# Stick-breaking attention on one core: scores of two heads issued in turn, transposed weights copied by ScalarE, last exponential one step earlier

## The chip, the cores and the metric

The kernel runs on one core of a Trainium2 chip. Time is the device time of one execution in microseconds. TensorE is PE in the profile (its weight loads are PEld), VectorE is DVE, ScalarE is ACT, GpSimd is POOL, and SyncE (SP) only starts transfers. Each engine takes its instructions strictly in the order in which the program left them, and waits on semaphores for what others make.

## The reference, cut to what matters

A decoder trunk of two layers over 1024 tokens of width 1024. Layer 0 mixes an S5 state-space block and eight heads of stick-breaking attention (head size 64); layer 1 has a pooling mixer; both have a large MLP and a gated embedding. Only the attention of layer 0 is touched by the change:

```
z = einsum("bhqd,bhkd->bhqk", qb, kf) * scale          # 128 queries of one block
causal = key_pos[None, :] < q_pos[:, None]
log_beta = log_sigmoid(z)
log_1m_beta = where(causal, log_sigmoid(-z), 0)
tail = cumsum(log_1m_beta, axis=keys, reverse=True) - log_1m_beta
w = where(causal, exp(log_beta + tail), 0)
out = einsum("bhqk,bhkd->bhqd", w, v)
```

So each row of a block of 128 queries needs a running sum over its keys from the right, between two exponentials and a logarithm. What precedes attention makes q, k and v; what follows multiplies its output by the second half of the output weights.

## The kernel before

Nearly all matrix products are split: an fp32 operand becomes a high part (rounded to the fp32r form, by ScalarE, L446) and a low part (VectorE subtracts, L450), and three products replace one (L477). This makes TensorE, VectorE and ScalarE all busy throughout.

Attention (`attention`, L661) is a list of **units**. The tokens have two halves `hf` of 512, each with four blocks `i` of 128 queries; heads come in four pairs. In the first half a unit is both heads of a pair for one block (16 units, up to 512 keys for each head). In the second half a unit is a single head (32 units, 640 to 1024 keys). A unit passes through five stages:

- `scores` (L670): TensorE multiplies q and k into PSUM banks of 512 columns (L682), adds the causal mask in the last bank (L686), ScalarE copies each bank into the tile `zs` (L687); VectorE then makes -|z| in `na` (L688) and max(z, 0) in `rz` (L689).
- `softplus` (L692): ScalarE takes exp and log of `na` (L694, L695), VectorE runs the reversed running sum over it into `rz` (L698).
- `weights` (L700): VectorE subtracts `rz` from `zs` (L702), ScalarE takes the exponential (L703): the attention weights.
- `turned` (L705): TensorE transposes the weights, 128 columns at a time, four to a PSUM bank of the tag `b` (L712), and VectorE copies each bank into the old `na` tile (L713).
- `values` (L715): TensorE multiplies the transposed weights with v (L730), both heads in turn.

The loop at L735 sets how the stages of successive units overlap: in step n it issues `values` of unit n-4, `weights` and `turned` of unit n-3, `softplus` of n-1, `scores` of n, with a `yield` after `turned`, one after `scores` and one more. At each yield other work may be woven in (`weave`, L1404): the rest of the projections, the GLU of S5, the two halves of the output projection and a first slice of the MLP. The order that results is handed to a scheduler that keeps each engine's list but places instructions by its own estimate of when they can run; what stands in the lists is shown below, since it follows from the code only loosely.

A head has 64 rows, so its score product uses the upper or the lower half of TensorE's rows: `rows = slice(64 * o, 64 * o + 64)`. PSUM banks for scores come from the tags `z` (two banks) and, in the second half, `st` (one). The tiles `zs` and `na` share a pool of eight buffers (`at`), `rz` one of four (`wq`), the transposed weights wait in two banks `b`. Other work uses these pools too: `wq` and `at` take weights and activations of the next stages.

## Time and profile before

| | |
|---|---|
| runs of the kernel before | 2160.73, 2167.41, 2173.29 us, median 2167.41 |
| the profiled execution | 2161.73 us; its span from first to last instruction 2159.9 us |
| busy over the span | PE 2072.2 us, PEld 1624.3, DVE 1838.9, ACT 1142.2, POOL 132.1 |
| instructions | PE 9464, DVE 2443, ACT 1613 |
| score matmuls (L682) | first at 262.6 us, last at 594.6 us |
| copies of transposed weights (L713) | 88, from 281.0 to 618.8 us |

Attention thus lies between about 260 and 622 us, a sixth of the span. Before and after it the kernel is projections, MLP and pooling. A row of the profile names line, engine, operation and tiles (`b<-ident,zs`: written tile, then the tiles read), shapes, count, and then busy time and mean duration. The mean of a PE row holds the pipeline's latency, so two matmuls that follow each other overlap in it: what a matmul costs TensorE is the distance of its start to that of the next. A wait is written with the instruction that ended it. `PEclk` is the share of its full clock that TensorE was granted.

### The profile page before, as it was taken

The page shows a single profiled execution, that of the slowest core. Times are in us where ns is not written, and L with a number is a line of the kernel's source. Part 1 is how long each engine was busy: PE and PEld are TensorE (multiplying, and loading weights), DVE is VectorE, ACT ScalarE, POOL GpSimd, SP SyncE. Part 2 cuts the span into 40 slices and gives each one's busy share as a digit, 9 for nine tenths or more (in the row PEclk, how much of TensorE's full clock was granted, in tenths as well). Part 3 has the DMA queues.
Part 4 walks back from the last instruction along what each step waited for, and adds up shares of the span by engine and source line. Part 5 has one row for each costly group of instructions (what it writes and reads, how often), then busy time and mean ns, then how long its engine had stood idle before and what let it go on. Part 6 is the DMA issues. An engine that isn't in the chain of part 4 may idle for free.

```text
span 2159.9 us, 24772 instructions
## 1 busy us (share of the span) xinstructions
PE 2072.2 (96%) x9464; PEld 1624.3 (75%) x9464; DVE 1838.9 (85%) x2443; ACT 1142.2 (53%) x1613; POOL 132.1 (6%) x263
## 2 busy tenths in 40 slices
PE   7899999989998999999999999888999999999997
PEld 5676766656577888888888887566888888888886
DVE  8866578978879888998878978999697998879998
ACT  5133466756644563756356555533654656365662
POOL 3856000000000000000000000000000000000000
PEclk9998999989899999999999999998999999999999
DMA  4111111220024112102202122322111201211221
GB/s 151 55 55 55 55 49 32 71 83 30 15 76 138 37 59 69 59 30 78 78 8 71 59 88 69 98 77 99 59 48 41 79 33 56 78 54 34 69 69 59
DMA packets 44742, 136.25 MB, mean 63 GB/s; under 512 B 9552, under 2 KB 10704, under 8 KB 44624
## 3 DMA queue, kind: packets, MB, share of 16 engines
q1 hardware_dynamic: 44624, 134.67, 18.6%
q8 instruction: 74, 1.21, 0.2%
q14 instruction: 44, 0.36, 0.1%
HBM read 129.28 MB, written 4.19 MB: 62 GB/s over the span
## 4 chain that ended last, share of the span: by engine, by line
PE 75%; DVE 19%; ACT 3%; issue 2%; DMA 1%; POOL 0%; SPq 0%; DVEq 0%; ACTq 0%
PE mm L477 27%; PE z L477 15%; PE b L477 12%; PE av L477 6%; PE st L477 6%; DVE rz L698 2%; DVE X L863 2%; DVE w L450 2%; PE z L682 1%; PE av L730 1%; PE b L712 1%; PE z L428 1%; DVE xgl L529 1%; DVE acc L499 1%; DVE na L713 1%
## 5 line engine op out<-in xcount | busy, mean ns | idle before, releaser
L477 PE MATMUL mm<-xgh,w 128*128 128x512 f32 x912 | 300.0, 405 | 15.5 <-ACT w L446 6.2
L450 DVE TENSOR_TENSOR w<-q,w 128x1024 fp32r<-128x1024 f32 x204 | 246.8, 1217 | 0.3 <-ACT w L446 0.3
L446 ACT CAST w<-q 128x1024 fp32r<-128x1024 f32 x204 | 212.8, 1047 | 29.0 <-PE mm L477 14.8
L477 PEld LDWEIGHTS mm<-xgh,w 128*128 128x128 f32 x912 | 173.1, 192 | 62.5 <-issue 9.1
L446 ACT CAST hsh<-H 128x1024 fp32r<-128x1024 f32 x98 | 102.3, 1047 | 197.1 <-PE st L477 88.5
L477 PE MATMUL mm<-xgl,w 128*128 128x512 f32 x456 | 183.0, 401 | 0.0
L446 ACT CAST w<-wr 128x1024 fp32r<-128x1024 f32 x98 | 102.3, 1047 | 150.1 <-PE mm L477 97.9
L477 PE MATMUL z<-xsh,w 128*128 128x512 f32 x576 | 177.7, 390 | 0.0
L863 DVE TENSOR_TENSOR q<-q,q 128x1024 f32<-128x1024 f32 x114 | 137.0, 1219 | 14.0 <-DMA q<-in_w_down 9.5
L450 DVE TENSOR_TENSOR w<-wr,w 128x1024 fp32r<-128x1024 f32 x98 | 128.1, 1312 | 21.1 <-ACT w L446 9.7
L477 PE MATMUL mm<-hsh,w 128*128 128x512 f32 x448 | 137.9, 389 | 0.0
L477 PE MATMUL b<-xsh,w 128*128 128x512 f32 x448 | 137.9, 389 | 0.0
L450 DVE TENSOR_TENSOR hsl<-H,hsh 128x1024 fp32r<-128x1024 f32 x98 | 119.4, 1219 | 11.4 <-ACT hsh L446 11.3
L446 ACT CAST xsh<-X 128x1024 fp32r<-128x1024 f32 x72 | 75.6, 1050 | 98.2 <-PE st L477 51.2
L477 PEld LDWEIGHTS z<-xsh,w 128*128 128x128 f32 x576 | 108.1, 188 | 22.9 <-issue 0.5
L477 PE MATMUL mm<-xsh,w 128*128 128x512 f32 x400 | 123.8, 389 | 0.0
L450 DVE TENSOR_TENSOR xsl<-X,xsh 128x1024 fp32r<-128x1024 f32 x72 | 87.4, 1220 | 38.7 <-ACT xsh L446 38.2
L477 PE MATMUL z<-xsl,w 128*128 128x512 f32 x288 | 112.1, 389 | 0.0
L450 DVE TENSOR_TENSOR xsl<-xt,xsh 128x512 fp32r<-128x512 f32 x108 | 70.1, 685 | 42.5 <-ACT xsh L446 42.5
L477 PEld LDWEIGHTS mm<-xgl,w 128*128 128x128 f32 x456 | 87.9, 193 | 21.8 <-issue 4.1
L477 PE MATMUL b<-hsh,w 128*128 128x512 f32 x336 | 103.6, 389 | 0.0
L477 PE MATMUL z<-hsh,w 128*128 128x512 f32 x336 | 103.4, 389 | 0.0
(360 smaller groups left out, 4874.5 us busy)
## 6 DMA issues: line engine op xcount, KB each, us to landing
q<-in_w_up SPq DMA_DIRECT2D x56, 512.0 KB, 3.6
q<-in_w_down SPq DMA_DIRECT2D x56, 512.0 KB, 3.7
wr<-in_w_in SPq DMA_DIRECT2D x26, 512.0 KB, 3.6
wr<-in_w_out SPq DMA_DIRECT2D x16, 512.0 KB, 3.5
wr<-in_w_up SPq DMA_DIRECT2D x16, 512.0 KB, 3.5
wr<-in_w_down SPq DMA_DIRECT2D x16, 512.0 KB, 3.5
x<-in_x SPq DMA_DIRECT2D x15, 512.0 KB, 5.7
wr<-in_w_gate SPq DMA_DIRECT2D x15, 512.0 KB, 3.5
```

The source lines that it names most:

```text
L428: nc.tensor.matmul(py[:, m], X[rows, ri, m, :], ca[rows, 2 * m + ri].rearrange("p j h -> p (j h)"), start=False, stop=(ri == 1))
L446: nc.scalar.copy(out=hi, in_=src)
L450: e.tensor_tensor(out=lo, in0=src, in1=hi.bitcast(F32), op=ALU.subtract)
L477: self.nc.tensor.matmul(ps, a, b, start=(first and n == 0 and i == 0), stop=(last and n == K - 1 and i == 2), skip_group_check=going)
L499: e.tensor_tensor(out=self.acc[hf], in0=self.acc[hf], in1=sq, op=ALU.add)
L529: self.nc.vector.scalar_tensor_tensor(out=lo, in0=x, scalar=g, in1=hi.bitcast(F32), op0=ALU.mult, op1=ALU.subtract)
L682: nc.tensor.matmul(pz[:, 0:b1 - b0], self.q[hf][pair // 2][rows, pair % 2, i * P:(i + 1) * P], self.k[b0 // HT][pair // 2][rows, pair % 2, ...
L698: v.tensor_tensor_scan(out=rz[:, rev], data0=na[:, rev], data1=rz[:, rev], initial=0.0, op0=ALU.add, op1=ALU.add)
L712: nc.tensor.transpose(pt[:, (kb - k0) * P:(kb - k0 + 1) * P], zs[:, kb * P:(kb + 1) * P], self.ident)
L713: v.tensor_copy(out=wT[:, k0 * P:k1 * P], in_=pt[:, 0:(k1 - k0) * P])
L730: nc.tensor.matmul(self.avp[64 * o:64 * o + 64, i * P:(i + 1) * P], self.v[kb // 4 * 2 + pair // 2][:, kb % 4, cs], w[:, at * P:(at + 1) * ...
L863: (self.nc.vector if eng == "v" else self.nc.gpsimd).tensor_tensor(out=o, in0=a, in1=b, op=op)
```

## The change

Three things change in `attention`, for the 48 units in all; the arithmetic stays the same.

1. In the second half, `scores` now takes the units of both heads at once. For each bank of 512 keys the matmul of head 0 and that of head 1 are issued one after the other, as the first half did already. It is called in the step of head 0, so head 1's scores are issued one step earlier than before.
2. The copies out of the transposes' banks (`turned`) go to ScalarE instead of VectorE.
3. The stages are issued in another order: `turned` of unit n-3, a yield, then in the second half `values` of the pair n-4 and n-3 as soon as its second head is turned, `weights` of n-2 (before: n-3), `softplus` of n-1, `scores`. In the first half `values` of n-4 still opens the step.

```
-        def scores(unit):
-            hf, pair, i, hs = unit
+        def scores(new):
+
+            hf, pair, i, _ = new[0]
             N = (4 * hf + i + 1) * P
-            zs, na = (self.a([P, SEQ], nm)[:, 0:len(hs) * N] for nm in ("zs", "na"))
-            rz = self.t([P, SEQ], "wq", name="rz")[:, 0:len(hs) * N]
+            heads = []
+            for unit in new:
+                W = len(unit[3]) * N
+                zs, na = (self.a([P, SEQ], nm)[:, 0:W] for nm in ("zs", "na"))
+                state[unit] = zs, na, self.t([P, SEQ], "wq", name="rz")[:, 0:W], N
+                heads += [(o, zs[:, n * N:(n + 1) * N]) for n, o in enumerate(unit[3])]
             for b0 in range(0, N, HT):
...
-                pzs = [self.p([P, HT], next(banks[hf])) for _ in hs]
+                pzs = [self.p([P, HT], next(banks[hf])) for _ in heads]
...
-                for n, pz in enumerate(pzs):
+                for pz, (_, zs) in zip(pzs, heads):
...
-                    nc.scalar.copy(out=zs[:, n * N + b0:n * N + b1], in_=pz[:, 0:b1 - b0])
+                    nc.scalar.copy(out=zs[:, b0:b1], in_=pz[:, 0:b1 - b0])
...
         def turned(unit):
...
-                v.tensor_copy(out=wT[:, k0 * P:k1 * P], in_=pt[:, 0:(k1 - k0) * P])
+                nc.scalar.copy(out=wT[:, k0 * P:k1 * P], in_=pt[:, 0:(k1 - k0) * P])
...
-        stages = (scores, 0), (softplus, 1), (weights, 3), (turned, 3), (values, 4)
-        for n in range(len(units) + stages[-1][1]):
-            for stage, lag in sorted(stages, key=lambda x: -x[1]):
-                if 0 <= n - lag < len(units):
-                    stage(units[n - lag])
-                if stage in (scores, turned):
-                    yield
+        for n in range(len(units) + 4):
+            back = lambda lag: units[n - lag] if 0 <= n - lag < len(units) else (None, None, None, None)
+            if back(4)[0] == 0:
+                values([back(4)])
+            if back(3)[0] is not None:
+                turned(back(3))
+            yield
+            if back(3)[0] == 1 and back(3)[3] == (1,):
+                values([back(4), back(3)])
+            if back(2)[0] is not None:
+                weights(back(2))
+            if back(1)[0] is not None:
+                softplus(back(1))
+            if back(0)[0] == 0:
+                scores([back(0)])
+            elif back(0)[3] == (0,):
+                scores([back(0), back(-1)])
+            yield
             yield
```

The lines behind it move: scores L682 to L686, masks L686 to L690, score copies L687 to L691, `na` and `rz` L688 and L689 to L694 and L695, exp and log L694 and L695 to L699 and L700, running sum L698 to L703, subtraction L702 to L707, last exponential L703 to L708, transposes L712 to L717, their copies L713 to L718, values L730 to L733.

**TensorE, second unit pair of the second half** (block i = 1, 768 keys). `z_` and `st_` are score banks, `b_` banks of transposes, `zs_` weights to be transposed. Before, with head 0 in the first two rows and head 1 in the eighth:

```order
L682 MATMUL z_3243<-k_778,q_2495 128x512
L682 MATMUL st_3246<-k_1790,q_2495 128x256
L686 MATMUL st_3246<-maskb,identb 128x128
L477 MATMUL mm_3252<-Yph_3096,w_2886 128x512
L712 MATMUL b_3225<-ident,zs_3083 128x128 x4
...
L730 MATMUL av_3125<-na_3084,v_1083 64x128 x8
L682 MATMUL z_3296<-k_778,q_2495 128x512
L712 MATMUL b_3281<-ident,zs_3140 128x128 x4
L712 MATMUL b_3287<-ident,zs_3140 128x128
L682 MATMUL z_3299<-k_1790,q_2495 128x256
```

Now:

```order
L686 MATMUL z_3248<-k_778,q_2495 128x512
L686 MATMUL st_3249<-k_778,q_2495 128x512
L717 MATMUL b_3225<-ident,zs_3085 128x128 x4
L717 MATMUL b_3231<-ident,zs_3085 128x128 x4
L686 MATMUL z_3254<-k_1790,q_2495 128x256
L690 MATMUL z_3254<-maskb,identb 128x128
...
L733 MATMUL av_3127<-na_3086,v_1083 64x128 x8
L717 MATMUL b_3293<-ident,zs_3142 128x128 x4
L717 MATMUL b_3299<-ident,zs_3142 128x128
L686 MATMUL z_3255<-k_1790,q_2495 128x256
```

The 512-key matmuls of both heads have come together; head 1's 256-key matmul has stayed a gemm and a set of transposes behind that of head 0.

**TensorE, seventh unit pair** (i = 2, 896 keys), now:

```order
L686 MATMUL z_3959<-k_778,q_2495 128x512
L717 MATMUL b_3928<-ident,zs_3595 128x128 x4
L717 MATMUL b_3934<-ident,zs_3595 128x128
L686 MATMUL z_3960<-k_778,q_2495 128x512
L686 MATMUL st_3965<-k_1790,q_2495 128x384
L690 MATMUL st_3965<-maskb,identb 128x128
L686 MATMUL z_3966<-k_1790,q_2495 128x384
```

Here five transposes stand between the two 512-key matmuls, but head 1's (z_3960) is followed by head 0's 384-key one (st_3965). Over all 16 pairs of the second half, the two 512-key matmuls of the first bank are neighbours in five; in three more, head 1's first bank has head 0's second 512-key matmul behind it; in three it is a 128-, 256- or 384-key matmul that has the other head's as its neighbour.

**ScalarE, during the output projection of the first half**, one pair of units. `zs_` from `z_` or `st_` are score copies, `na_` from `b_` the new copies. Before:

```order
L687 COPY zs_4208<-z_4211 128x512
L687 COPY zs_4208<-z_4214 128x256
L703 ACTIVATE zs_4064<-zs_4064 128x1024
L703 ACTIVATE zs_4117<-zs_4117 128x640
L694 ACTIVATE na_4209<-na_4209 128x768
L528 ACTIVATE xgh_3918<-x_3402,gain 128x512
L446 CAST avh_3332<-av_3952 128x512
L695 ACTIVATE na_4209<-na_4209 128x768
L687 COPY zs_4252<-st_4255 128x512
L687 COPY zs_4252<-z_4258 128x256
```

Now:

```order
L718 COPY na_4042<-b_4193 128x512
L718 COPY na_4042<-b_4199 128x512
L700 ACTIVATE na_4137<-na_4137 128x640
L691 COPY zs_4228<-z_4234 128x512
L708 ACTIVATE zs_4133<-zs_4133 128x640
L691 COPY zs_4231<-z_4235 128x512
L446 CAST avh_3317<-av_3937 128x512
L691 COPY zs_4228<-st_4240 128x256
L691 COPY zs_4231<-z_4241 128x256
L718 COPY na_4134<-b_4252 128x512
L718 COPY na_4134<-b_4258 128x128
L708 ACTIVATE zs_4136<-zs_4136 128x640
```

The copies out of the transposes stand among the score copies and the exponentials, and the exponential of a unit (zs_4133) is followed by four other instructions before the copies of its transposes (na_4134).

More of the change, by code (lines that the diff above doesn't have):

```diff
@@ L677, in scores @@
                 last = b1 == N
-                pzs = [self.p([P, HT], next(banks[hf])) for _ in hs]
-                for pz, o in zip(pzs, hs):
+                pzs = [self.p([P, HT], next(banks[hf])) for _ in heads]
+                for pz, (o, _) in zip(pzs, heads):
                     rows = slice(64 * o, 64 * o + 64)
@@ L712, in turned, with values @@
                     nc.tensor.transpose(pt[:, (kb - k0) * P:(kb - k0 + 1) * P], zs[:, kb * P:(kb + 1) * P], self.ident)
-                v.tensor_copy(out=wT[:, k0 * P:k1 * P], in_=pt[:, 0:(k1 - k0) * P])
-        def values(unit):
-            hf, pair, i, hs = unit
-            if hs == (0,):
-                return
+                nc.scalar.copy(out=wT[:, k0 * P:k1 * P], in_=pt[:, 0:(k1 - k0) * P])
+        def values(done):
+            hf, pair, i, _ = done[0]
             nk = 4 * hf + i + 1
@@ L724, in values @@
                     self.av[hf] += self.act(2, "av")
-            wT = [state.pop((hf, pair, i, x))[1] for x in (((0, 1),) if hs == (0, 1) else ((0,), (1,)))]
+            wT = [state.pop(unit)[1] for unit in done]
             for kb in range(nk):
```

7 lines of the change are left out of this document (4 added, 3 removed).

## The prediction

> **What bounds the kernel now.** I began with the page's busy line, which only says that three engines are nearly full on average:
>
> ```profile
> PE 2072.2 (96%) x9464; PEld 1624.3 (75%) x9464; DVE 1838.9 (85%) x2443; ACT 1142.2 (53%) x1613; POOL 132.1 (6%) x263
> ```
>
> Attention is a sixth of the span, so next came the busy time of each engine by stretch. I cut at the places where the kernel changes: the first half's attention (from 240 us), the GLU and S5's output projection with the second half's attention (341.3 to 469), a stretch of gemms alone, then the output projection and MLP slice with the rest of attention (493.65 to 622).
>
> ```profile
> core 0: us, PE busy (x) PEld busy (x) DVE busy (x) ACT busy (x) POOL busy (x), PEclk, DMA share, GB/s
> 240.00:341.30 101.30, 94.85 (x489) 64.27 (x487) 74.81 (x119) 62.20 (x99) 4.21 (x2) 1.00 0.16 53
> 341.30:469.00 127.70, 119.50 (x612) 75.30 (x611) 117.14 (x156) 89.72 (x134) 0.00 (x0) 0.93 0.17 58
> 469.00:493.65 24.65, 24.65 (x118) 20.20 (x118) 13.99 (x17) 5.17 (x6) 0.00 (x0) 0.96 0.20 68
> 493.65:622.00 128.35, 121.94 (x698) 79.27 (x695) 116.66 (x151) 83.42 (x124) 0.00 (x0) 0.95 0.08 26
> 622.00:690.00 68.00, 63.99 (x272) 51.68 (x271) 58.02 (x77) 26.56 (x37) 0.00 (x0) 0.97 0.38 131
> ```
>
> Call the second row stretch I and the fourth stretch II. VectorE is busy for 117.14 of 127.70 us (0.917) and 116.66 of 128.35 us (0.909), ScalarE for 0.70 and 0.65. TensorE's busy time counts latency, so its fullness must be read elsewhere: from who waits for whom, in both stretches together (the columns are total, times, longest):
>
> ```profile
> ACT na L694 <- DVE na L688: 21.5, 14, 4.3
> ACT zs L703 <- DVE zs L702: 20.7, 11, 4.5
> ACT w L446 <- PE mm L477: 13.8, 4, 4.4
> DVE na L713 <- PE b L712: 12.8, 11, 3.3
> PEld b L712 <- ACT zs L703: 12.7, 11, 4.2
> PEld av L730 <- DVE na L713: 10.6, 14, 1.9
> ACT zs L687 <- PE av L730: 9.4, 5, 3.2
> ACT avh L446 <- PE av L730: 9.2, 4, 3.6
> PE b L712 <- ACT zs L703: 6.8, 4, 3.4
> ACT zs L687 <- PE z L686: 5.8, 4, 2.7
> ACT zs L687 <- PE b L712: 5.8, 3, 3.2
> ACT mixh L446 <- PE z L682: 4.0, 2, 3.3
> ACT zs L687 <- PE st L682: 3.9, 1, 3.9
> ```
>
> ScalarE waits mostly for VectorE (42.2 us in the first two rows); TensorE's transposes wait for the last exponential, its `values` for VectorE's copies. The chain of waits in I and in II agrees that no engine alone sets the pace:
>
> ```profile
> by line: PE mm L477 16.7%; DVE rz L698 10.5%; issue 8.7%; PE z L682 8.5%; PE b L712 8.0%; PE av L730 5.2%; DVE w L450 4.6%; DVE na L713 4.5%; DVE rz L689 4.1%; DVE mixl L450 4.0%; DVE zs L702 3.6%; DVE na L688 3.4%; ACT zs L703 3.1%; PE st
> by line: PE mm L477 28.4%; PE av L730 12.7%; PE z L682 11.7%; DVE rz L698 10.2%; PE b L712 8.3%; PE st L682 6.7%; DVE na L713 5.8%; issue 3.0%; DVE zs L702 2.9%; DVE na L688 1.7%; DVE rz L689 1.7%; ACT zs L703 1.4%; PE z L686 1.1%; DVE acc
> ```
>
> It passes between TensorE and VectorE, and VectorE is the fullest. One place shows what a late exponential costs (start, length, what, wait before it):
>
> ```profile
> 447.43 1.12 PE L682 MATMUL z<-k,q 64*128 64x512 f32 x2
> 451.92 1.54 PE L712 MATMUL b<-ident,zs 128*128 128x128 f32 x6 [3.36 <-ACT zs L703]
> 454.19 2.07 PE L682 MATMUL st<-k,q 64*128 64x512 f32 x2 [0.73 <-ACT zs L687]
> 451.90:465.60 13.70, 12.28 (x32) 6.72 (x33) 8.83 (x12) 7.88 (x11) 0.00 (x0) 0.56 0.00 0
> 574.90:588.60 13.70, 13.70 (x47) 8.86 (x46) 10.15 (x14) 7.16 (x11) 0.00 (x0) 0.56 0.12 39
> ```
>
> After 3.36 us of waiting the same score product takes 2.07 us in place of 1.12, and the granted clock is 0.56 over 13.70 us; in II there is a second such window. Each costs TensorE 13.70 x 0.44 = 6.0 us of full-speed work.
>
> **The change, part by part.** *Copies to ScalarE.* 88 copies go. By stretch, VectorE's time in them, and what a copy of 128x512 costs on either engine:
>
> ```profile
> 240.00:341.30 101.30, 5.70 (x10) 1.00 0.16 53
> 341.30:469.00 127.70, 22.05 (x40) 0.93 0.17 58
> 493.65:622.00 128.35, 21.00 (x38) 0.95 0.08 26
> L713 DVE COPY na<-b 128x512 f32<-128x512 f32 x56 | 37.3, 684 | 13.6 <-PE b L712 13.5
> L687 ACT COPY zs<-z 128x512 f32<-128x512 f32 x35 | 20.0, 580 | 15.4 <-PE av L730 5.9 <-PE b L712 4.1 <-PE z L686 4.0
> ```
>
> ScalarE has no such copy from a `b` bank yet, but its score copies have the same shape and go the same way, PSUM to SBUF: 580/684 = 0.85 of VectorE's price. So VectorE falls to 117.14 - 22.05 = 95.1 us in I and 116.66 - 21.00 = 95.7 in II; ScalarE rises by 18.7 to 108.4 and by 17.8 to 101.2 us. The fullest engine changes: ScalarE instead of VectorE, with 8.7 and 15.5 us less work than VectorE has now.
>
> The score copies by the same two stretches (ScalarE's time in them) are 40 and 34:
>
> ```profile
> 341.30:469.00 127.70, 18.31 (x40) 0.93 0.17 58
> 493.65:622.00 128.35, 16.77 (x34) 0.95 0.08 26
> ```
>
> *Scores in turn.* The first half shows what neighbours do, four matmul records being two heads in two passes each; a single head of the same 512 keys stands below:
>
> ```profile
> 276.89 1.15 PE L682 MATMUL z<-k,q 64*128 64x512 f32 x4
> 277.98 0.23 PE L686 MATMUL z<-maskb,identb 128*128 128x128 bf16 x1
> 532.04 1.12 PE L682 MATMUL z<-k,q 64*128 64x512 f32 x2
> 533.10 0.23 PE L686 MATMUL z<-maskb,identb 128*128 128x128 bf16 x1
> ```
>
> Both heads take 1.09 us start to next start, one head alone 1.06: the two run side by side, and a pair of neighbours saves 1.03 us. But the lists above show neighbours of 512 columns in only 8 of the 16 pairs (five in the first bank, three with the second), and three smaller ones. I count 8 x 1.03 = 8.2 us and, in proportion to columns, about 1.5 for the others: 10 us less work for TensorE. Had all stood together, it would be 16 pairs of on average 832 columns for each head, 16 x 1.03 x 832/512 = 27 us. Head 1's scores come a step earlier, which holds a second pair of `zs` and `na`: eight buffers for two pairs, as many as there are. Where they don't suffice, ScalarE's score copies wait for `values` to release them, as they do now for 9.4 us.
>
> *The last exponential earlier.* It stands a step ahead of its transposes instead of right before them. The 12.7 us in which weight loads waited for it (6.8 of them in front of idle matmuls) should mostly go. What is late next is the copy behind the transposes, now in ScalarE's list: behind it stand the next scores' copies and exponentials, and for these wait VectorE's sums.
>
> *Transfers.* In SP's list the loads of the second half of x move behind two more loads of output weights; those need weight buffers that are split while the first half is projected. What reads x comes after 469 us, so I price this at nothing; cover gone, it would cost the loads' own few us.
>
> *First half.* Ten copies before 341.3 us: VectorE 5.7 us less, ScalarE 4.8 more at 62 of 101 us. Bounds -5.7 and +4.8; I take 0, since neither engine is over 0.75 there.
>
> *Sum.* The best that ScalarE can do as the fullest engine is what VectorE does now: 108.4/0.917 = 118.2 and 101.2/0.909 = 111.3 us, 26.5 us less than today. The other end: ScalarE's waits for TensorE (the seven rows above, 13.8 + 9.4 + 9.2 + 5.8 + 5.8 + 4.0 + 3.9 = 51.9 us) all stay, and only those for VectorE go; then the two stretches take 209.6 + 51.9 = 261.5 us, 5.5 more than the 256.05 of now. If moreover each of the 78 new copies waits for TensorE as long as a score copy (24.9 us over the 74 in I and II, 0.34 each), 26 more, 31.8 in all. I take a fill of 0.88, near the upper end, because transposes that don't wait for an exponential and 10 us less score work make TensorE earlier, but below it, because VectorE (95) and TensorE are now close behind ScalarE: 108.4/0.88 = 123.2 (-4.5) and 101.2/0.88 = 115.0 (-13.4). Together -17.9: 2161.73 becomes 2143.8 us. The profiled execution is the second lowest of the four; the runs' median is 5.7 higher, and I add half of that: **2147 us**.
>
> **The rivals.** *ScalarE blocks (slower).* One mechanism: in ScalarE's list a copy waits for transposes, which wait in TensorE's list behind gemms; meanwhile the exponentials behind it stand still and VectorE starves. It decides once ScalarE waits for more than 256.05 - 209.6 = 46.4 us in I and II. For it speaks that it waits 51.9 us for TensorE today; against, that TensorE itself gets earlier. Price between +5.5 and +31.8, middle +18.6: 2183 with the same 2.9 added. The Trainium skill, "TensorEngine Tiling (Array Packing)", section "PSUM Bottleneck", speaks for this rival: tiling speeds TensorE up but not the emptying of PSUM, and both ScalarE and VectorE should be used for that, whereas here all of attention's banks now fall to ScalarE. The trace agrees as far as it goes: VectorE's 43 us of copies are a fifth of its work in I and II.
>
> *Only exchanged (no change).* VectorE's copies hold 4.5% and 5.8% of the chain, 13.2 us; in their place come ScalarE's at 0.85, 11 us, and the running sums stay. Then 2161.73 + 2.9, about 2165. Against it: VectorE loses 43 us of work where it was over 0.9 full.
>
> *Everything fits (a larger gain).* VectorE's fill of 0.917 and 0.909 contains the slow-clock windows. Without them it would be 117.14/121.7 = 0.96 and 116.66/122.35 = 0.95. If the early exponential removes what led to both, and ScalarE fills as well, I takes 112.9 and II 106.5 us: 36.6 less, 2128 us. The Trainium skill, "TensorE: Matmul & The Clock Gate", section "HAM oscillation — how this bites in real kernels", asks for no idle gap over about 3.4 us; the first window had a gap of 3.36 us, the trace agrees. By that rule the second window, ahead of which no gap of that length stands, wouldn't go with it, and this rival would give 6.0 us less.
>
> **How the numbers follow.** Forecast 0.55; everything fits 0.18; only exchanged 0.15; ScalarE blocks 0.12. The forecast's own range is 2132 to 2158. With the larger gain below and the first steps of blocking above, the range is **2122 to 2172**; that leaves out the worst of blocking and gains beyond 45 us. A measurement of this kernel tells about 0.5%, 10.8 us, from no change. Faster by more than that: nearly all of the forecast and the larger gain, 0.69. Within it: the exchange, and small gains and losses of the others, 0.20. Slower: 0.11.
>
> **What would show it.** Right: in the profile after, VectorE near 95 us in each of the two stretches, ScalarE near 105, both stretches shorter, II by more; the new copies at about 580 ns; few waits of transposes for the last exponential; fewer or shorter windows at half clock; score products of neighbours at 1.09 us. ScalarE's waits for TensorE in both stretches together stay below 46 us. Wrong: ScalarE's copies from the transposes wait for TensorE, VectorE's row for `na` or the running sum waits for ScalarE, and the stretches don't shrink; or a new long gap on TensorE brings back the low clock. Anything that moves outside 240 to 690 us would be a cause that I haven't seen.

## The result: 0.55% faster, by another route than forecast

The changed kernel takes 2152.69 us (median of 14 runs, 2148.7 to 2161.87), the kernel before 2169.34 us beside it (14 runs, 2160.72 to 2177.27). The ratio is 0.9945, 95% interval 0.9929 to 0.996. A second comparison, on another occasion, gave 2152.06 against 2165.7 us, ratio 0.9933 (0.991 to 0.9956). The forecast was 2147 us, range 2122 to 2172.

### The profile after, by the same stretches

The stretches are cut at the same products of the large gemms in every kernel (line 477; the cuts of before move by under 1 us against those of the prediction). First the kernel before: the stretch ahead of attention, the first half's attention, stretch I and stretch II. Columns as in the prediction: window, length, busy time and instructions of PE, PEld, DVE, ACT and POOL, granted clock, share of the DMA engines, GB/s.

```profile
0.00:240.12 240.12, 218.07 (x1071) 163.46 (x1071) 175.97 (x388) 81.88 (x126) 127.04 (x253) 0.96 0.24 79
240.12:341.92 101.80, 95.35 (x490) 64.39 (x488) 75.23 (x119) 62.79 (x100) 4.21 (x2) 1.00 0.16 52
341.92:469.29 127.37, 119.17 (x610) 75.32 (x610) 116.89 (x155) 89.14 (x132) 0.00 (x0) 0.93 0.17 58
...
494.02:622.03 128.01, 121.59 (x693) 79.07 (x691) 116.69 (x151) 83.05 (x124) 0.00 (x0) 0.95 0.08 25
```

The same of the changed kernel, profiled execution of 2160.36 us:

```profile
0.00:248.03 248.03, 227.61 (x1070) 169.63 (x1071) 172.68 (x388) 82.00 (x126) 126.49 (x253) 0.91 0.24 76
248.03:352.04 104.01, 99.43 (x489) 67.87 (x487) 70.27 (x109) 66.32 (x110) 4.19 (x2) 0.95 0.16 51
352.04:485.05 133.01, 117.31 (x617) 74.16 (x617) 101.88 (x119) 107.05 (x177) 0.00 (x0) 0.90 0.17 56
...
509.60:620.82 111.22, 107.85 (x685) 73.46 (x684) 98.41 (x112) 96.50 (x159) 0.00 (x0) 1.00 0.09 33
```

And of a second profiled execution of the changed kernel (span 2150.3 us):

```profile
0.00:238.38 238.38, 216.91 (x1070) 163.25 (x1071) 178.01 (x388) 82.01 (x126) 126.24 (x253) 0.96 0.25 79
...
340.80:475.14 134.34, 119.55 (x617) 75.17 (x617) 101.81 (x119) 107.27 (x177) 0.00 (x0) 0.88 0.17 55
...
499.68:610.91 111.23, 107.84 (x685) 73.47 (x684) 98.42 (x112) 96.58 (x159) 0.00 (x0) 1.00 0.10 33
```

Three things are to be seen. *First*, 7.9 us of the first changed profile are lost ahead of 240 us, where TensorE gets the same work in both programs: the granted clock is 0.91 there and 0.96 in the other two. That belongs to the execution, not to the change. Whoever compares the two spans, 2159.9 and 2158.5, without the stretches finds a gain of 1.4 us. *Second*, stretch II is 16.8 us shorter, in both profiles. *Third*, stretch I is 5.6 and 7.0 us longer, although VectorE has 15 us less work there. From the first cut at 240 us to the gemms alone at 690 us the two changed profiles are 7.7 and 8.0 us shorter; the medians lie further apart (16.7 and 13.6 us), and the profiled execution of before is itself at the low end of its runs.

The granted clock splits these numbers. Half-clock time costs TensorE half of itself (length x (1 - PEclk): stretch I of before 127.4 x 0.07 = 9). Taken off, by the clock's own records, an estimate of what the work takes at full clock is left:

| us | first half: length, lost | I: length, lost | II: length, lost | all three | lost | rest |
|---|---|---|---|---|---|---|
| before | 101.8, 0.0 | 127.4, 9.5 | 128.0, 6.8 | 357.2 | 16.3 | 340.9 |
| changed | 104.0, 5.1 | 133.0, 13.1 | 111.2, 0.0 | 348.2 | 18.2 | 330.0 |
| changed, second profile | 102.4, 3.4 | 134.3, 16.5 | 111.2, 0.0 | 348.0 | 19.9 | 328.1 |

So the work itself became 11 to 13 us shorter, and in these two profiles 2 to 4 us of it went back in half-clock time. By stretch the rest is 101.8, 117.9 and 121.2 us before, 98.9, 119.9 and 111.2 after (second profile 99.0, 117.8, 111.2): at full clock too, I gained nothing.

The second comparison has span and mean clock of each of its runs, and with them the same split of whole executions: span times clock is 2112.0 us before and 2098.7 after (medians of 14 and 9 runs), the lost part 53.0 and 51.6. So over the runs the work is 13 us shorter, and none of it goes back; the profiled execution of before lost only 44.1 us. The clock of a run is given to three digits, which is 1.1 us on a run. Among the runs of before, one that loses 10 us more also shows about 3 us less rest, so half clock costs a little less than half of itself, and a kernel that loses much looks some us too short in the rest.

The waits of both stretches together, changed kernel (total, times, longest), beside those in the prediction:

```profile
ACT w L446 <- PE mm L477: 19.0, 5, 4.7
...
DVE rz L703 <- ACT na L700: 15.0, 13, 1.6
ACT zs L708 <- DVE zs L707: 13.6, 18, 2.3
PEld b L717 <- ACT zs L708: 12.2, 10, 5.2
...
ACT na L718 <- PE b L717: 9.4, 7, 4.1
PE b L717 <- ACT zs L708: 8.3, 5, 5.0
DVE na L694 <- ACT zs L691: 7.7, 3, 3.9
...
DVE na L694 <- PE b L717: 5.0, 2, 4.2
```

ScalarE waited 42.2 us for VectorE; the row of 21.5 us is gone and that of 20.7 is 13.6. In their place VectorE waits for ScalarE's logarithms (15.0) and score copies (7.7). Of the 19.0 us in which ScalarE waits for gemms (`ACT w <- PE mm`) all but 1.2 lie in the stretch of gemms between I and II, as did all 13.8 before. But the transposes wait for the last exponential as long as before: 12.2 us (12.7), 8.3 in front of idle matmuls (6.8). The chain of waits in I and in II says the same: no engine alone, with ScalarE's steps now in it.

```profile
by line: PE mm L477 20.7%; DVE rz L703 12.9%; PE z L686 10.5%; PE b L717 7.6%; PE av L733 5.4%; issue 5.1%; ACT na L700 4.2%; ACT na L718 4.0%; DVE zs L707 3.9%; ACT zs L691 3.9%; ACT na L699 3.5%; ACT zs L708 3.1%; DVE mixl L450 2.9%; PE s
by line: DVE rz L703 20.3%; PE mm L477 9.2%; DVE zs L707 9.0%; ACT na L699 8.6%; ACT zs L708 7.5%; issue 6.4%; ACT na L700 5.1%; ACT zs L691 4.3%; ACT na L718 4.2%; PE av L733 4.0%; DVE xgl L529 2.4%; PE b L717 2.4%; DVE acc L499 2.2%; DVE 
```

Where stretch I loses, the timeline of the changed kernel shows one place, in rows picked from two engines (start, length, what, wait before it):

```profile
467.30 1.20 PE L477 MATMUL mm<-mixh,w 128*128 128x512 f32 x4 [1.20 <-ACT mixh L446]
468.34 0.82 PE L717 MATMUL b<-ident,zs 128*128 128x128 f32 x6
469.26 0.63 DVE L694 TENSOR_SCALAR na<-zs 128x896 int32<-128x896 int32 x1 [4.23 <-PE b L717]
470.02 2.02 DVE L703 TENSOR_TENSOR_SCAN rz<-na,rz 128x896 f32<-128x896 f32 x1
...
474.20 1.75 PE L717 MATMUL b<-ident,zs 128*128 128x128 f32 x7 [4.99 <-ACT zs L708]
```

Transposes stand in TensorE's list behind a gemm that waits for ScalarE's cast `mixh`; the `na` of the next scores waits for these transposes, by the program's pools most likely for the buffer that they free, so VectorE stands for 4.23 us; its sum, the subtraction and the exponential follow, and the next transposes wait 4.99 us. The second profile has the same gap at the same unit.

### The profile page after: what moved, and what is told of

Same layout as the page of the kernel before. It is cut to its first block, busy times and chain, and to the rows that moved or that the text cites. A ratio compares the mean times of both kernels' runs of the same rounds, so it can differ in the third digit from the quotient of the medians.

```text
span 2158.5 us, 24768 instructions
## 1 busy us (share of the span) xinstructions
PE 2072.4 (96%) x9464; PEld 1629.4 (75%) x9464; DVE 1794.8 (83%) x2355; ACT 1175.3 (54%) x1701; POOL 131.6 (6%) x263
## 4 chain that ended last, share of the span: by engine, by line
PE 74%; DVE 18%; ACT 5%; issue 2%; POOL 1%; DMA 0%; SPq 0%; DVEq 0%; ACTq 0%; POOLq 0%
PE mm L477 28%; PE z L477 15%; PE b L477 12%; PE av L477 6%; PE st L477 6%; DVE rz L703 2%; DVE w L450 2%; DVE X L877 2%; PE z L428 1%; DVE xgl L529 1%; DVE zs L707 1%; PE z L686 1%; DVE acc L499 1%; ACT na L699 1%; DVE H L1039 1%
## 5 line engine op out<-in xcount | busy, mean ns | idle before, releaser
L477 PE MATMUL mm<-xgh,w 128*128 128x512 f32 x912 | 304.1, 410 | 14.8 <-ACT w L446 6.2
L446 ACT CAST w<-q 128x1024 fp32r<-128x1024 f32 x204 | 212.8, 1047 | 29.1 <-DVE q L877 18.7
L446 ACT CAST w<-wr 128x1024 fp32r<-128x1024 f32 x98 | 102.5, 1048 | 155.0 <-PE mm L477 108.4
L450 DVE TENSOR_TENSOR w<-wr,w 128x1024 fp32r<-128x1024 f32 x98 | 124.6, 1276 | 25.9 <-PE mm L477 13.2
L450 DVE TENSOR_TENSOR hsl<-H,hsh 128x1024 fp32r<-128x1024 f32 x98 | 119.3, 1218 | 12.0 <-ACT hsh L446 11.9
L446 ACT CAST xsh<-X 128x1024 fp32r<-128x1024 f32 x72 | 75.6, 1050 | 98.3 <-PE st L477 51.3
L703 DVE TENSOR_TENSOR_SCAN rz<-na,rz 128x128 f32<-128x128 f32 (+7 forms) x64 | 84.9, 1348 | 24.1 <-ACT na L700 23.8
L528 ACT ACTIVATE xgh<-x,gain 128x512 fp32r<-128x512 f32 x80 | 57.3, 719 | 85.9 <-DVE x L1310 28.6
```

What stands on the lines that cost most here:

```text
L446: nc.scalar.copy(out=hi, in_=src)
L450: e.tensor_tensor(out=lo, in0=src, in1=hi.bitcast(F32), op=ALU.subtract)
L477: self.nc.tensor.matmul(ps, a, b, start=(first and n == 0 and i == 0), stop=(last and n == K - 1 and i == 2), skip_group_check=going)
L528: self.nc.scalar.activation(out=hi, in_=x, func=AF.Copy, scale=g)
L703: v.tensor_tensor_scan(out=rz[:, rev], data0=na[:, rev], data1=rz[:, rev], initial=0.0, op0=ALU.add, op1=ALU.add)
```

## The experiments

Of each kernel only the rows that decide are shown, by stretch and in the columns of the first section unless said otherwise; a table at the end of the section has all kernels.

### Each part undone

**The copies back on VectorE.**

```diff
-                nc.scalar.copy(out=wT[:, k0 * P:k1 * P], in_=pt[:, 0:(k1 - k0) * P])
+                v.tensor_copy(out=wT[:, k0 * P:k1 * P], in_=pt[:, 0:(k1 - k0) * P])
```

> The change with its copies of the transposed weights given back to VectorE; paired scores and early exponential stay. If the copies carry the gain (my forecast: VectorE was the fullest engine and lost 43 us of work), VectorE is at 117 us in each of the two stretches again and nearly all of the gain of 16.7 us goes: ratio to before 0.998 to 1.002, about 2168 us. If the pairs or the early exponential carry it, 10 us or more of the gain stay: ratio below 0.9955.

Measured: 2166.16 us, ratio 1.0001 (0.9982 to 1.0019). The whole gain is gone. Stretches I and II, with paired scores and the early exponential but VectorE full again:

```profile
352.75:485.00 132.25, 116.51 (x618) 74.34 (x617) 120.23 (x159) 90.75 (x135) 0.00 (x0) 0.91 0.17 56
509.55:633.86 124.31, 112.36 (x686) 76.95 (x684) 115.59 (x148) 82.46 (x122) 0.00 (x0) 0.95 0.09 29
```

Stretch II takes 124.3 us in place of 111.2. Without the copies the rest of the change gains nothing in time: at full clock it shortens II by 3.7 us (121.2 to 117.5) and lengthens I by 3.0 (117.9 to 120.9).

**The scores one head after the other.**

```diff
-            if back(0)[0] == 0:
+            if back(0)[0] is not None:
                 scores([back(0)])
-            elif back(0)[3] == (0,):
-                scores([back(0), back(-1)])
```

> The change with the two heads' scores issued one after the other again, each in its own step; copies on ScalarE and the early exponential stay. If the pairs matter as I counted them (10 us less TensorE work), the time is 5 to 10 us above the change, ratio to before 0.997 to 0.999. If the second pair of score buffers costs as much as the pairs save (VectorE stood still for 4.2 us behind transposes at 465 us of the changed profile), the ratio stays at 0.9945 or falls below.

Measured: 2151.61 us, ratio 0.9935 (0.991 to 0.996), the same as with pairs. The stretches show that this is a balance and not nothing:

```profile
354.90:484.78 129.88, 123.68 (x611) 76.16 (x611) 99.25 (x116) 104.72 (x172) 0.00 (x0) 0.88 0.17 57
509.89:624.50 114.61, 113.82 (x692) 76.29 (x691) 98.56 (x113) 98.25 (x162) 0.00 (x0) 1.00 0.09 30
```

In II the pairs gain 3.4 us (114.6 against 111.2), in I they cost 3.1 to 4.5 (129.9 against 133.0 and 134.3). At full clock it is 3.4 in II and 3.9 to 6.0 in I. Part of the cost in I is work that has moved: with pairs, 6 matmuls and 5 ScalarE instructions more fall into I, and 7 and 3 fewer into II.

**The last exponential back before its transposes.**

```diff
             if back(3)[0] is not None:
+                weights(back(3))
                 turned(back(3))
...
-            if back(2)[0] is not None:
-                weights(back(2))
```

> The change with the last exponential back right before its transposes. If the early exponential matters, the transposes' waits for it (12.7 us before) return and the time is 5 us or more above the change: ratio to before 0.997 or more. If the waits only move from the exponential to the copy behind the transposes, the ratio stays within 0.9935 to 0.9955.

Measured: 2154.3 us, ratio 0.9935 (0.991 to 0.996). The ratio is the second expectation's, but its waits hardly move: in both stretches weight loads of transposes wait 14.3 us for the exponential (12.2 with the change), those of `values` 10.2 us for the copies (11.1). Stretches I and II are within 1.5 us of the change's:

```profile
340.81:474.24 133.43, 116.76 (x616) 75.21 (x616) 99.86 (x117) 106.35 (x175) 0.00 (x0) 0.89 0.16 56
498.40:611.09 112.69, 107.38 (x688) 74.38 (x686) 98.53 (x112) 96.42 (x159) 0.00 (x0) 0.98 0.10 32
```

**The second head's buffers taken a step later.** Only the scores of the second head are made early; `na` and `rz`, and the two operations that fill them, follow in its own step.

```diff
-                zs, na = (self.a([P, SEQ], nm)[:, 0:W] for nm in ("zs", "na"))
-                state[unit] = zs, na, self.t([P, SEQ], "wq", name="rz")[:, 0:W], N
+                zs = self.a([P, SEQ], "zs")[:, 0:W]
+                state[unit] = zs, N
...
+        def signs(unit):
...
+                na = self.a([P, SEQ], "na")[:, 0:W]
+                rz = self.t([P, SEQ], "wq", name="rz")[:, 0:W]
...
+            if back(0)[0] is not None:
+                signs(back(0))
```

> The change, but the second head of a pair takes its buffers for na and rz, and VectorE's two operations that fill them, one step later; only its scores are taken early. If the buffers hold VectorE back (waits of the sign operation for transposes, 12.7 us in the first stretch of the changed profile), these waits fall below 4 us and the time falls by 3 to 8 us below the change: ratio to before 0.991 to 0.993. If the buffers are not what costs, the ratio stays at 0.9945, or rises because the second head's sums start later.

Measured: 2160.73 us, ratio 0.996 (0.994 to 0.998), slower than the change. The waits in stretch I show that the experiment didn't take away what it was to take away (line 699 is here the operation of 694, line 722 that of 717):

```profile
DVE na L699 <- ACT zs L691: 10.7, 2, 7.3
...
DVE na L699 <- PE b L722: 5.0, 2, 4.5
```

The 5.0 us behind transposes are still there, and 10.7 us of waiting for score copies (7.7 before the edit) came on top. Whether the buffers alone cause the loss in I stays open; a kernel with more than eight of them wasn't tried.

### The copies alone, split and doubled

**Only the copies.** The kernel before with one line changed.

```diff
-                v.tensor_copy(out=wT[:, k0 * P:k1 * P], in_=pt[:, 0:(k1 - k0) * P])
+                nc.scalar.copy(out=wT[:, k0 * P:k1 * P], in_=pt[:, 0:(k1 - k0) * P])
```

> The kernel before with one line changed: the copies of the transposed weights go to ScalarE; scores, last exponential and the order of the stages stay as before. If the copies alone carry the gain (giving them back took all of it, undoing the pairs or the early exponential took nothing), the ratio to before is 0.992 to 0.9955. If they pay only together with one of the other two (each of which could stand in for the other when one was undone), the ratio is 0.997 or more.

Measured: 2167.01 us (2155.61 to 2176.38), ratio 1.0007 (0.9988 to 1.0026): no gain, though giving back the copies took all of it. The rows tell why:

```profile
241.42:349.31 107.89, 101.99 (x490) 69.66 (x488) 69.97 (x109) 66.48 (x110) 4.19 (x2) 0.92 0.15 50
349.31:489.48 140.17, 133.07 (x610) 80.48 (x610) 99.39 (x116) 105.94 (x173) 0.00 (x0) 0.81 0.16 53
513.97:628.75 114.78, 113.58 (x692) 76.25 (x691) 99.10 (x113) 98.77 (x163) 0.00 (x0) 1.00 0.09 32
```

Stretch II has 13.2 us of gain, but I runs at a clock of 0.81: 26.8 us lost there, 8.5 more in the first half. At full clock the three stretches would take 327.5 us, as little as with the whole change; TensorE's half clock takes all of it back. This is not one profile alone: over the 12 runs span times clock is 2098.8 us (2113.6 in the kernel before beside them), and 66.0 us are lost (49.8). So the copies bring the work's gain, and something else in the change keeps the clock. With the pairs undone, or the early exponential undone, the runs lose 50.5 and 53.8 us, so neither is needed if the other is there. But both of those kernels also issue the second half's `values` earlier than the kernel before, and this one doesn't: that this alone keeps the clock was not tested.

**Copies split.** The second bank's copy (keys from 512 on) back on VectorE.

```diff
-                nc.scalar.copy(out=wT[:, k0 * P:k1 * P], in_=pt[:, 0:(k1 - k0) * P])
+                (v.tensor_copy if k0 % 8 else nc.scalar.copy)(out=wT[:, k0 * P:k1 * P], in_=pt[:, 0:(k1 - k0) * P])
```

> The change with the copy of each second bank (keys from 512 on, 38% of the columns in the second half) back on VectorE; the first bank's stays on ScalarE. If ScalarE sets the pace now (107 of 133 and 96 of 111 us busy), 14 us less work there make it 5 to 14 us faster than the change, ratio 0.988 to 0.992. If VectorE's relief is what counts, 38% of the gain is lost: 6 us slower than the change, ratio 0.997. If neither engine sets the pace alone, 0.993 to 0.995.

Measured: 2160.14 us, ratio 0.9968 (0.995 to 0.9985). The number is that of the second theory, 38% of the gain lost. By the table below its rest (328.1) is no worse than the change's, and what is lost is clock (23.0), so the number alone doesn't show the theory. ScalarE has only 9 us less work in I and II (102.1 and 92.4 us), VectorE 14 more (109.2 and 105.1). That ScalarE alone sets the pace doesn't fit: the kernel would have become faster.

**Copies doubled.** Every copy is made twice on ScalarE.

```diff
-                nc.scalar.copy(out=wT[:, k0 * P:k1 * P], in_=pt[:, 0:(k1 - k0) * P])
+                for _ in range(2):
+                    nc.scalar.copy(out=wT[:, k0 * P:k1 * P], in_=pt[:, 0:(k1 - k0) * P])
```

> The change with every copy of the transposed weights made twice on ScalarE: some 37 us of ScalarE work more in the two stretches, nothing else. If ScalarE as the fullest engine sets the pace (my forecast's model, work divided by a fill of 0.88), the time rises by about 37/0.88 = 42 us: ratio to before 1.013. If the stretches are set by the chain through several engines, of which ScalarE's copies are a part, by 10 to 25 us: ratio 0.999 to 1.006. If ScalarE's copies lie beside other work, under 5 us.

Measured: 2179.6 us, ratio 1.0066 (1.0044 to 1.0089), 27 us above the change. Between the two theories' numbers:

```profile
343.85:490.30 146.45, 125.68 (x608) 78.05 (x607) 102.22 (x118) 122.17 (x214) 0.00 (x0) 0.81 0.15 51
515.00:639.03 124.03, 113.08 (x662) 75.08 (x661) 98.21 (x112) 111.43 (x197) 0.00 (x0) 0.96 0.08 25
```

ScalarE has 30.1 us more work in I and II (122.17 + 111.43 against 107.05 + 96.50), so the first theory would give 30.1/0.88 = 34 us; the three stretches are 26 us longer than in the change's profile. Of these only 7.3 us are longer work (337.3 against 330.0), 18.7 are half clock (36.9 against 18.2). All 7.3 us and a little more come in II (111.2 to 118.9 at full clock); in I, with 15 us of ScalarE work added, the rest didn't grow (119.9 and 118.1), and the cost is half clock alone. So ScalarE doesn't set the pace of I; what its delays cost there is clock.

### A faster version, and tests of the cause

**Pairs in the second stretch only.** The first two pairs of heads are scored one after the other, the last two in turn.

```diff
-            if back(0)[0] == 0:
+            if back(0)[0] == 0 or back(0)[0] == 1 and back(0)[1] < 2:
                 scores([back(0)])
             elif back(0)[3] == (0,):
```

> The change with the scores of the first two pairs of heads issued one after the other and those of the last two in turn. In the first stretch the pairs seemed to cost (133.0 us with them, 129.9 without), in the second to gain (111.2 and 114.6). If that is so, this kernel has the better of both: 3 us below either, ratio to before 0.991 to 0.9925. If the difference lies only in where half-clock windows fell, the ratio is that of the two, 0.9935 to 0.9945.

Measured: 2145.12 us, ratio 0.9923 (0.9901 to 0.9945). Repeated beside the next two:

> The kernel with late pairs unchanged, beside the other two on the same chip: ratio to before 0.990 to 0.9945 as measured; its half-clock windows show how much these move from one execution to the next.

Measured: 2147.83 us, ratio 0.9931 (0.9907 to 0.9955). The stretches are those that the expectation put together, in both profiles (here the first):

```profile
339.34:468.11 128.77, 122.11 (x611) 75.66 (x610) 97.78 (x115) 104.66 (x172) 0.00 (x0) 0.89 0.17 58
492.97:604.26 111.29, 108.68 (x692) 73.96 (x691) 98.83 (x113) 98.46 (x163) 0.00 (x0) 1.00 0.10 33
```

Its medians are 4 to 8 us below those of the change; the intervals of the ratios overlap, so a gain over the change is likely but not shown. Span times clock points the same way: 15.8 and 16.5 us below the kernel before, with the change 13.3. Against the kernel before the gain is shown.

**TensorE kept busy in three gaps.** In that kernel the three longest waits of transposes in I were these; half clock began at 385.37 and at 450.22 us, so the second wait reaches into it and the third lies in it:

```profile
385.23 1.23 PE L717 MATMUL b<-ident,zs 128*128 128x128 f32 x5 [0.94 <-ACT zs L708]
...
450.70 1.54 PE L717 MATMUL b<-ident,zs 128*128 128x128 f32 x6 [1.14 <-ACT zs L708]
454.35 1.54 PE L717 MATMUL b<-ident,zs 128*128 128x128 f32 x6 [2.10 <-ACT zs L708]
```

```diff
+        fill = {(1, 0, 0, (1,)): 4, (1, 1, 1, (0,)): 5, (1, 1, 1, (1,)): 9}
...
                 pt = self.p([P, HT], "b")
+                for _ in range(fill.get(unit, 0) if k0 == 0 else 0):
+                    nc.tensor.matmul(pt[:, 0:P], self.identb, self.maskb, start=True, stop=True)
```

> The kernel with late pairs, and at the three places where its transposes waited longest for an exponential in the first stretch (0.94, 1.14 and 2.10 us idle, ahead of half-clock windows of 13.7 us each at 385 and 450 us) TensorE first makes 4, 5 and 9 products of 0.23 us into the bank that the transposes then overwrite: 4.1 us of work that nobody needs. If idle time in a grid window is what takes the clock, the half-clock time of the first stretch falls from 27.3 to at most 10 us and the time by 3 to 9 us below late pairs: ratio to before 0.988 to 0.991. If the clock falls for another reason, the 4 us are lost or hidden: ratio 0.9923 to 0.994.

Measured: 2148.96 us, ratio 0.9922 (0.9903 to 0.9941): no faster than late pairs. In the profiled execution stretch I was shorter:

```profile
341.51:465.52 124.01, 116.43 (x628) 72.99 (x628) 97.56 (x115) 104.32 (x172) 0.00 (x0) 0.96 0.18 60
```

It takes 124.0 us in place of 128.8 and 129.0, at a clock of 0.96 in place of 0.89, with 10.2 us at half clock in place of 27.3. The window at 385 us is gone, the one at 450 has stayed. The added products took far less than the expectation's 4.1 us: its 0.23 us is the length of one record, and in a row they overlap. These are the three rows:

```profile
386.07 0.40 PE L718 MATMUL b<-maskb,identb 128*128 128x128 bf16 x4
...
445.31 0.45 PE L718 MATMUL b<-maskb,identb 128*128 128x128 bf16 x5
...
449.65 1.12 PE L718 MATMUL b<-maskb,identb 128*128 128x128 bf16 x9 [0.46 <-ACT na L721]
```

That is 2.0 us in all, and 0.61, 0.50 and 1.01 us of the three waits are left. Nor do the runs show the profile's gain: the profiled one lost 38.5 us to half clock, the least of the six; their median is 49.4, that of late pairs beside them 47.2. That work which keeps TensorE busy holds the clock is therefore not shown; a run that fills the waits whole is missing.

**Transposes last in a step.** In the late-pairs kernel, the two exponentials of other units go ahead of the transposes.

```diff
+            if back(2)[0] is not None:
+                weights(back(2))
+            if back(1)[0] is not None:
+                softplus(back(1))
             if back(3)[0] is not None:
                 turned(back(3))
             yield
             if back(3)[0] == 1 and back(3)[3] == (1,):
                 values([back(4), back(3)])
-            if back(2)[0] is not None:
-                weights(back(2))
-            if back(1)[0] is not None:
-                softplus(back(1))
```

> The kernel with late pairs, and in each step the exponentials of the other two units stand ahead of the transposes and their copies, not behind. With late pairs VectorE's running sums waited 22.1 us for ScalarE's logarithms in the first stretch, and ScalarE's copies 8.3 us for transposes. If ScalarE's list blocks (my slower rival, in part), the 22.1 us fall below 12 and the time by 3 to 8 us: ratio to before 0.988 to 0.991. If ScalarE is simply full, the waits change places and the ratio stays at 0.992 to 0.994; if the transposes now come too late for values, it rises above that.

Measured: 2160.22 us, ratio 0.9984 (0.9968 to 1.0), 12 us slower than late pairs. VectorE's wait for the logarithms hardly fell (22.1 before the edit), and stretch I was at half clock for 47 us:

```profile
DVE rz L703 <- ACT na L700: 20.9, 13, 5.4
```

```profile
350.41:488.89 138.48, 130.72 (x614) 80.01 (x613) 100.22 (x116) 105.36 (x173) 0.00 (x0) 0.83 0.16 54
```

But this doesn't clear the copies. Between its exponential and its logarithm, 8 of 19 units of stretch I now have a copy in ScalarE's list, where with late pairs 2 had one, and at one of the longest waits a copy blocks as before. First late pairs, then this kernel:

```profile
398.04 0.86 ACT L718 COPY na<-b 128x512 f32<-128x512 f32 x2 [4.79 <-PE b L717]
398.79 0.97 ACT L700 ACTIVATE na<-na 128x896 f32<-128x896 f32 x1
399.78 2.02 DVE L703 TENSOR_TENSOR_SCAN rz<-na,rz 128x896 f32<-128x896 f32 x1 [4.33 <-ACT na L700]
...
409.12 0.59 ACT L718 COPY na<-b 128x512 f32<-128x512 f32 x1 [4.15 <-PE b L717]
409.60 0.95 ACT L700 ACTIVATE na<-na 128x896 f32<-128x896 f32 x1
410.59 2.03 DVE L703 TENSOR_TENSOR_SCAN rz<-na,rz 128x896 f32<-128x896 f32 x1 [3.68 <-ACT na L700]
```

The copy waits for transposes, the logarithm stands behind it, and VectorE's sum waits for the logarithm. At this place 4 of the 22 us are caused by a copy ahead in the list; for the others it stays open.

**The change again.**

> The change itself, a second time. Ratio to before 0.993 to 0.996 as measured. In its first profile 7.9 us were lost ahead of 240 us, where the two programs do the same, in half-clock windows; if these belong to the execution and not to the change, they can be absent here. If the gain belongs to the second stretch, that takes 111 to 112 us again; if the first stretch's loss belongs to the change, it takes 130 us or more again, with half-clock windows of 20 us or more.

Its numbers and rows stand in the first section: 0.9933, none of the 7.9 us lost ahead of 240 us, stretch II at 111.2 and stretch I at 134.3 us with 33 us of half clock.

### All of them

First half, I and II, worked out as above from the profiles; the last two columns are from the runs, medians less those of the kernel before beside them:

| kernel | ratio to before | three stretches | lost to half clock | rest | rest of first half, I, II | runs: lost | runs: span times clock |
|---|---|---|---|---|---|---|---|
| before | 1 | 357.2 | 16.3 | 340.9 | 101.8, 117.9, 121.2 | 0 | 0 |
| copies on VectorE, rest as the change | 1.0001 | 361.0 | 21.6 | 339.4 | 101.1, 120.9, 117.5 | +4.3 | -0.8 |
| only copies on ScalarE | 1.0007 | 362.8 | 35.3 | 327.5 | 99.4, 113.4, 114.8 | +16.3 | -14.8 |
| the change | 0.9945 | 348.2 | 18.2 | 330.0 | 98.9, 119.9, 111.2 | not on record | not on record |
| the change again | 0.9933 | 348.0 | 19.9 | 328.1 | 99.0, 117.8, 111.2 | -1.4 | -13.3 |
| without pairs | 0.9935 | 351.3 | 24.5 | 326.9 | 98.3, 113.9, 114.6 | -1.4 | -11.0 |
| without the early exponential | 0.9935 | 346.6 | 17.0 | 329.6 | 100.5, 118.1, 111.0 | +1.9 | -13.2 |
| late buffers | 0.996 | 351.3 | 21.4 | 329.8 | 99.1, 119.4, 111.4 | +9.6 | -13.6 |
| copies split | 0.9968 | 351.1 | 23.0 | 328.1 | 99.9, 116.5, 111.7 | +8.5 | -12.7 |
| copies doubled | 1.0066 | 374.2 | 36.9 | 337.3 | 100.3, 118.1, 118.9 | +21.0 | -4.9 |
| late pairs | 0.9923 | 339.4 | 13.7 | 325.7 | 99.3, 115.1, 111.3 | -4.8 | -15.8 |
| late pairs again | 0.9931 | 342.8 | 17.1 | 325.7 | 99.0, 115.4, 111.4 | -0.3 | -16.5 |
| late pairs, gaps filled | 0.9922 | 337.8 | 8.5 | 329.3 | 99.1, 118.9, 111.3 | +1.9 | -15.7 |
| transposes last | 0.9984 | 354.3 | 27.2 | 327.2 | 99.0, 114.7, 113.4 | +11.9 | -15.9 |

The rest has two groups: about 340 with the copies on VectorE, 326 to 330 with them on ScalarE (337 when doubled), and the last column says the same over the runs. What else the kernels differ in is mostly the time lost. By stretch, the copies alone take 4.5 us off I and 6.4 off II at full clock. In II the pairs take off 3.3 to 3.7 more, whichever way the copies go; in I they add 2 to 6 us, part of it moved work. Copies on ScalarE with the early exponential but without pairs (98.3, 113.9, 114.6) and the copies alone (99.4, 113.4, 114.8) have nearly the same rest.

## Why the prediction held, point by point

**Copies to ScalarE: right, and nearly all of the shorter work.** Price: 580 ns expected, measured 592:

```profile
L718 ACT COPY na<-b 128x512 f32<-128x512 f32 x56 | 32.3, 592 | 11.9 <-PE b L717 11.8
```

ScalarE came to 107.05 and 96.50 us (108.4 and 101.2 expected), VectorE to 101.9 and 98.4 (95.1 and 95.7 expected; in I, 36 fewer instructions fall between the cuts, not the 40 of the copies, since four others, 4 us, have moved in). Undoing this part undid everything; alone it shortens the work as much as the change does, but not the time, since the clock takes it back.

**Scores in turn: mis-sized.** I counted 10 us less TensorE work. The neighbours are there (7 pairs of 512 keys run side by side in the first profile, 8 in the second, where I counted 8) and cost what was expected, 595.50 to 596.56 us for two heads:

```profile
595.50 0.69 PE L686 MATMUL z<-k,q 64*128 64x512 f32 x1
595.51 0.69 PE L686 MATMUL st<-k,q 64*128 64x512 f32 x1
...
596.56 0.23 PE L690 MATMUL st<-maskb,identb 128*128 128x128 bf16 x1
```

But TensorE wasn't the pace, so of the saved time 3.4 us show in II, and in I the pairs cost 3 to 4.5; whether by the buffers of the early second head is open. "Eight buffers for two pairs, as many as there are" was the right place to look; I expected ScalarE to wait there, and it was VectorE (4.23 us).

**The last exponential earlier: wrong.** The 12.7 us "should mostly go"; they are 12.2. In II the transposes' waits fell from 6.2 to 2.4, in I they rose from 6.4 to 9.8, half of it at the one place shown, where the exponential was late because the sum before it was. Undone, the time stays the same.

**The sum.** Forecast -4.5 in I and -13.4 in II. Measured +5.6 and +7.0 in I, -16.8 in both profiles in II. The step that failed is the one fill of 0.88 for both stretches: ScalarE is busy for 107.05/133.01 = 0.80 of I and 96.50/111.22 = 0.87 of II. That 0.87 comes near 0.88 in II is luck as far as the mechanism goes: split copies lower ScalarE's fill there to 92.42/115.13 = 0.80 without a gain. Of the 16.8 us, 6.8 are the half-clock window that went and 10.0 shorter work, about 6.4 by the copies and the rest by the pairs. In I the fill hides what is not work of ScalarE. The copies alone take 4.5 us off I at full clock, just the forecast; the pairs, which I had counted as a gain, take it back, with gemms for which TensorE's list makes attention wait (467 us) as one way that the trace shows; and half clock costs 3.6 and 7.0 us more than before (26 us of it in the first profile, lost 13.1). The total came close by luck, for two reasons: II made good a third of the error in I (-3.4 of +10), and the median of before lies 5.7 to 7.6 us above its profiled execution, of which I had added 2.9. Profile against profile the gain is 9.6 us at best (spans 2159.9 and 2150.3), median against median 13.6 to 16.7.

Three readings behind the sum were wrong. The 51.9 us of ScalarE's waits for TensorE contain 13.8 that lie wholly between 469 and 493.65 us, outside both stretches. Within them it is 38.1, so that end of the sum is 247.7 us, 8.4 less than 256.05 and not 5.5 more, and *ScalarE blocks* runs from -8.4 to +17.9. The two half-clock windows are 13.65 us long and cost 6.8 us each, not 6.0: they begin at 450.34 and 573.22 us, 1.6 us ahead of the cuts that gave a clock of 0.56. And the first of them begins 1.8 us into the wait of 3.36 us, which lasts from 448.56 to 451.92, so the clock did not fall after a gap of that length.

**The rivals.** *Everything fits* was right for II: its half-clock window, 6.8 us, went, and the clock is 1.00. It was wrong for I. Its sentence on the rule of the Trainium skill, by which the second window would not go, is contradicted: it went (below). *Only exchanged* fell: VectorE's copies on ScalarE shorten the rest by 11 to 13 us; with the copies alone its time came out (ratio 1.0007), but through the clock. *ScalarE blocks* put its condition at 46.4 us of waiting for TensorE; within I and II of the changed kernel ScalarE's waits for TensorE are 15.0 and 3.6 us. But its mechanism exists: with late pairs one copy waits 4.79 us for transposes and VectorE 4.33 behind it, and doubled copies cost 27 us for 30, more than two thirds of it through the clock. And the transfers, the loads of x and the time after 690 us were rightly priced at nothing: what follows the cut at 690 us takes 1468 to 1471 us in every kernel profiled.

## What to carry to other kernels

Compare two profiles of a kernel with such a clock by stretches that are cut at the same instructions, and take the half-clock time apart from the work, before any cause is named: here both spans were nearly equal, the work was 11 us shorter, and one edit alone gained 13 us of work and lost it all to the clock. Moving work from the fullest engine to another pays, but what it pays in time depends on the clock that TensorE then keeps: the doubled copies cost 7 us of work and 19 us of clock. And an interleaving that helps one stretch can cost another: try it by stretch.

## What the runs showed that I had not expected

**The clock seems to follow the share of the array that works, not the length of a gap.** The granted clock changes on a grid of 3.413 us (its stretches at half clock last 3.413, 6.827, 10.240, 13.653 us and so on). I laid that grid over 14 profiles (before, the change twice, the experiments) and worked out for each window how long any matmul ran, and the same with each matmul weighted by its tile's share of 128x128 (a score product of one head, 64*128, counts a half). Then how often the next window was at half clock:

| weighted activity of a window | at full clock: windows, next one half | at half clock: windows, next one half |
|---|---|---|
| under 0.2 | 93, 76 | 22, 22 |
| 0.2 to 0.4 | 105, 72 | 41, 41 |
| 0.4 to 0.55 | 228, 33 | 73, 73 |
| 0.55 to 0.65 | 338, 0 | 61, 61 |
| 0.65 to 0.8 | 520, 0 | 76, 62 |
| over 0.8 | 7089, 0 | 168, 3 |

No window over 0.55 was ever followed by a fall, and below 0.65 none was followed by a return. The durations are an estimate, the distance from start to next start at full clock (0.227 us for a product of 128x512, 0.53 for a score pass of 512 columns) and twice that at half clock; taken a little differently they move single counts (92 falls of 92 in the first row in place of 76 of 93, 8 of 269 in the third in place of 33 of 228, one return below 0.65), but not the border at 0.55. Without the weights it blurs: of 567 windows at full clock in which TensorE was busy for 0.55 to 0.8 of the time, 24 of the 125 with a weighted activity under 0.5 were followed by a fall, and none of the other 442. The window before the fall at 573 us in the kernel before had an activity of 0.19, with waits of 0.81 and 1.35 us and the first 0.2 of one of 1.26; those before the falls at 385 and 450 us with late pairs about 0.3 and 0.4, though TensorE was busy for about 0.6 and 0.75 of them, with scores of one head at a time. This is read from records; that single-head scores as such let the clock fall was not tested by a run of its own. The Trainium skill, "TensorE: Matmul & The Clock Gate", section "HAM oscillation — how this bites in real kernels", warns of idle gaps over about 3.4 us; here the longest wait in the window before the fall at 385 us was 0.94 us.

**The same program takes this differently from run to run.** The Trainium skill, same page, section "What's actually happening", calls the window free-running, so that its place in the kernel differs. The traces agree: the two profiles of the change lose 22.2 and 10.2 us ahead of 240 us with the same work. A difference of 8 us between single executions means nothing here.
